# Row pairs 0, 2, 4, 5 and 6 of each down product as seven block products, one weight sum by an accumulating GpSimd transfer

## The chip, the cores and the metric

The kernel runs on one core of a Trainium2 chip. The metric is the device time of one execution in microseconds (us). TensorE (PE) multiplies, VectorE (DVE) and ScalarE (ACT) do elementwise work, GpSimd (POOL) does a little of that and issues transfers, SyncE (SP) only issues transfers. Each engine works through its own queue in order and waits there on semaphores.

## The reference

One decoder layer for 256 tokens of width 1024, in float32: a gated FFN at half weight, a mixer of two attentions, a second gated FFN at half weight, a final norm.

```
h = x + 0.5 * swiglu(rms_norm(x, n1), gate1, up1, down1)     # hidden width 2816
h = h + hybrid_mixer(rms_norm(h, n2), ...)                   # w_in 1024 x 5120, two attentions, w_out
h = h + 0.5 * swiglu(rms_norm(h, n3), gate2, up2, down2)
out = rms_norm(h, final_norm)

swiglu(x, g, u, d) = (silu(x @ g) * (x @ u)) @ d
```

The case is about `(...) @ d`, the down product of each FFN: 256 x 2816 times 2816 x 1024.

## The kernel before

**Weights as a stream.** All weights come as 376 tiles of 128 x 512 float32, in the order in which they are used, two tiles to a chunk of 512 KB. SyncE loads chunks into four buffers (`raw`); a chunk's buffer is loaded anew when its last reader is done (`load`, L170, called at the end of `split`).

**Three matmuls a product.** A float32 product is made of two reduced parts for each factor: `wh` is the weight rounded to fp32r (ScalarE, L213 or with a gain L217), `wl` the rest (VectorE, L214 or L218). A product of a 128-token block and a weight tile is three matmuls, high by high, high by low, low by high (`mm3`, L353, and its lines 355 to 357). There are ten buffers for the pairs `wh`, `wl`.

**Splitting ahead.** After each product (`unit`, L359) the kernel calls `weave.tick()`, which gives the other tasks a step, and `W.pump()`, which splits at most one more weight. In a down product an item may be split when it is at most eight ahead of the item that TensorE uses (`AHEAD_DOWN`, 9), and when one of the ten buffers is free.

**Tasks in ticks.** A tick is one product. The activations of the hidden layer are transposed by VectorE in 32 x 32 squares, and 16 small transfers (`exchange`, L506) move the squares into place; some ticks later they are split into `hth` and `htl` (`turn_hidden`, L551). Blocks of hidden columns go in pairs p; the transfers for p = 4 and 5 are issued by GpSimd, the others by SyncE. So while the down product begins, GpSimd still issues the exchanges of the last two.

**Seven products for eight.** The down product takes the 22 rows of weight tiles in row pairs g = 0 to 10. A row pair is four tiles, B11, B12, B21, B22, and with two token blocks of two column blocks of activations it is a 2 x 2 by 2 x 2 block product: eight block products, or seven in Winograd's form. Pairs 0, 2, 4, 6 of each FFN use seven (`SEVENS`, L31), the others eight. For a seven, VectorE makes four sums of activations (L563 to L566, small, once for each pair, split into `c_f`) and four sums of weights, T3 to T6 (`seventh`, L187, its instruction L195):

```
T3 = B12 - B11,  T4 = B22 - B12,  T5 = B22 - T3,  T6 = B21 - T5
```

The seven weight operands are then B11, B21, B22, T3, T4, T5, T6, each split as any other weight: seven items where a plain row pair has four (each of these used twice). Their products go to X, (0,0), (0,1), V, Z, Y, (1,0) (`seven`, L656). X, Y, Z, V are summed over all sevens and added to h by VectorE after the last of them (`post`, L675, D_POST = 3 ticks later: L679 to L696, with ScalarE's copy of X at L683); the rest goes to the ordinary sums in PSUM.

**The order.** TensorE and SyncE run in the order of the program throughout. From the start to the end of the first FFN's down products (up to its last rows), and from early in the second FFN on, all engines do (`ordered`). Elsewhere a planner orders VectorE, ScalarE and GpSimd by its own costs. The first FFN ends with 7 rows (`TAILS`, 1: 7) that are taken for one half of the columns and then for the other, so that the residual (L652), the transposes of h (L431, `uq`), their exchange on GpSimd and SyncE and the split into `uh`, `ul` can run ahead of the mixer's first projection (`in`). The second FFN has the plain pairs 7 and 8 and a tail of 4 rows behind its last seven.

Of the kernel before, what the change touches and what calls it, by code (L numbers as in the profile page):

```python
# [8 lines left out]
F32 = mybir.dt.float32  # L9
# [18 lines left out]
NEG = -1e30  # L28
CH = 2
N_TILES = 376  # L30
SEVENS = (0, 2, 4, 6), (0, 2, 4, 6)  # L31
W_IN = FB * KD + 2 * KF + 3 * len(SEVENS[0])
W_BR = W_IN + 10 * KD
W_OUT = W_BR + 16
# [29 lines left out]
D_STICK = (7, 6, 6, 6)  # L64
AHEAD = 7
AHEAD_DOWN = 9


INV_FREQ = [
# [30 lines left out]
class Weave:  # L100


    def __init__(self):
        self.now = 0
        self.tasks = []
# [54 lines left out]
class Weights:  # L160


    def __init__(self, nc, pool, early, sums, stream, gain, bufs, ahead):
        self.early, self.sums, self.items = early, sums, _items()
        self.nc, self.pool, self.stream, self.gain = nc, pool, stream, gain
        self.bufs, self.ahead = bufs, ahead
        self.loaded = self.ready = self.freed = self.at = 0
        self.raw, self.parts, self.behind = {}, {}, {}

    def load(self, n, tiles=0):  # L170

        n = min(n, N_TILES // CH)
        while self.loaded < n * CH + tiles:
            c, j = divmod(self.loaded, CH)
            if j == 0:
                nm = f"raw{c}"
                self.raw[c] = self.early(nm) if c < 12 else self.pool.tile([P, CH * 512], F32, name=nm, tag="raw", bufs=4)
            step = 1 if c < 3 else CH
            s = slice(j * 512, (j + step) * 512)
            for piece in HALVES if self.loaded == 0 else (s,):  # L180
                self.nc.sync.dma_start(self.raw[c][:, piece], self.stream[c, :, piece])
            self.loaded += step

    def tile(self, s):
        return self.raw[s // CH][:, s % CH * 512:s % CH * 512 + 512]

    def seventh(self, s, j):  # L187

        if j < 4:
            if j == 0:  # L190
                self.made = {}
            a, b, o = ((1, 0, 3), (3, 1, 4), (3, 3, 5), (2, 5, 6))[j]
            self.made[o] = self.sums(f"T{s}_{o}")
            b = self.made[b] if j > 1 else self.tile(s + b)
            self.nc.vector.tensor_sub(self.made[o], self.tile(s + a), b)  # L195
        raw = self.made[j] if j > 2 else self.tile(s + (0, 2, 3)[j])
        return raw, {1: s // CH, 3: s // CH + 1}.get(j)

    def split(self):
        i = self.ready  # L200
        s, j = self.items[i]
        used = s // CH if s % CH == CH - 1 else None
        if j is None:
            self.load(s // CH + 1)
            raw = self.tile(s)
        else:
            self.load(s // CH + (2 if j else 1))
            raw, used = self.seventh(s, j)
        hi = self.pool.tile([P, 512], F32R, name=f"wh{i}", tag="wh", bufs=self.bufs)
        lo = self.pool.tile([P, 512], F32R, name=f"wl{i}", tag="wl", bufs=self.bufs)  # L210
        g = self.gain(i)
        if g is None:
            self.nc.scalar.copy(hi, raw)  # L213
            self.nc.vector.tensor_sub(lo, raw, hi.bitcast(F32))  # L214
        else:
            for s in HALVES if i == 0 else (slice(0, 512),):
                self.nc.scalar.activation(hi[:, s], raw[:, s], AF.Copy, scale=g)  # L217
                self.nc.vector.scalar_tensor_tensor(lo[:, s], raw[:, s], g, hi[:, s].bitcast(F32),  # L218
                                                    op0=ALU.mult, op1=ALU.subtract)
        self.parts[i] = hi, lo  # L220
        self.ready += 1
        if i in self.behind:
            self.behind.pop(i)()
        if used is not None:
            del self.raw[used]
            self.load(used + 1 + 4)
# [19 lines left out]
def hybrid_layer_kernel(ctx, tc, x, xt, pos, g_final, bgate, wstream, out):  # L246
# [19 lines left out]
    def big(nm, dt=F32R):  # L266
        return work.tile([P, 1024], dt, name=nm, tag="big", bufs=24)
# [7 lines left out]
    def row512(nm):  # L275
        return work.tile([P, 512], F32, name=nm, tag="tok", bufs=4)


    h = [consts.tile([P, D], F32, name=f"h{t}") for t in range(2)]
    first = consts.tile([P, 3 * KD + T], F32, name="first")  # L280
# [11 lines left out]
                return gk[:, n * KD + k:n * KD + k + 1]  # L292
        return None

    W = Weights(nc, wpool, lambda nm: big(nm, F32), row512, wstream, gain, WB, AHEAD0)

    xin = [big(f"xin{j}", F32) for j in range(2)]

# [112 lines left out]
    class Normed:  # L411
        def __init__(self, t, nm):
            self.t, self.nm = t, nm
            self.parts = big(f"{nm}h{t}"), big(f"{nm}l{t}")
            self.r = consts.tile([P, 1], F32, name=f"r_{nm}{t}")
            self.there = set()
# [112 lines left out]
    def ffn(base, xn, nm, on_half, lag, last=False):  # L529
# [21 lines left out]
        def turn_hidden(p, n):  # L551
            moved = big(f"hm_{nm}{p}", F32)
            yield from exchange(moved, squares[p], n, [nc.gpsimd if p > 3 else nc.sync], D_MOVE)
            yield D_MOVED
            hts[p] = big(f"hth_{nm}{p}"), big(f"htl_{nm}{p}")
            split(plain(hts[p][0][:, 0:n * P]), plain(hts[p][1][:, 0:n * P]), slots(moved, n))
            for g in range(2 * p, 2 * p + 2):
                if g in sevens:
                    a11, a21, a12, a22 = (slots(moved, n)[:, g % 2 * 4 + s] for s in range(4))
                    yield D_SUMS  # L560
                    raw = wide(f"cs_{nm}{g}", 512)
                    s1, s3, s2, s4 = (plain(raw)[:, s] for s in range(4))
                    nc.vector.tensor_add(s1, a21, a22)  # L563
                    nc.vector.tensor_sub(s3, a11, a21)
                    nc.vector.tensor_sub(s2, s1, a11)
                    nc.vector.tensor_sub(s4, a12, s2)  # L566
                    yield D_SUMS
                    both = big(f"c_{nm}{g}")
                    split(both[:, 0:512], both[:, 512:1024], raw)
                    crossed[g] = [[both[:, q * 512 + m * P:q * 512 + (m + 1) * P] for q in range(2)] for m in range(4)]  # L570
# [104 lines left out]
        def post():  # L675

            def add(t, c, src):
                s = slice(c * 512, c * 512 + 512)
                nc.vector.scalar_tensor_tensor(h[t][:, s], src, 0.5, h[t][:, s], op0=ALU.mult, op1=ALU.add)  # L679

            xs, w, r, wv = (row512(f"{q}_{nm}") for q in ("xs", "xy", "xyz", "xyv"))
            add(0, 0, common["X"])
            nc.scalar.copy(xs, common["X"])  # L683
            yield 1
            nc.vector.tensor_add(w, common["Y"], xs)
            yield 1
            nc.vector.tensor_add(r, common["Z"], w)
            yield 1
            add(1, 0, r)
            yield 1  # L690
            nc.vector.tensor_add(wv, common["V"], w)
            yield 1
            add(0, 1, wv)
            yield 1
            rv = row512(f"xyzv_{nm}")
            nc.vector.tensor_add(rv, common["V"], r)  # L696
            yield 1
            add(1, 1, rv)
# [564 lines left out]
```

## Time and profile before

| | |
|---|---|
| median of 3 runs | 548.29 us (548.05 to 548.39) |
| profiled execution, its own time | 548.34 us |
| its span, first to last instruction | 546.6 us |
| granted TensorE clock | 0.996 |
| TensorE busy | 99% |
| VectorE busy | 83% |
| ScalarE busy | 65% |
| GpSimd busy | 21% |
| moved by DMA | 112.23 MB, mean 205 GB/s |

How to read the lines of the profile. A group's line gives source line, engine, operation, output <- inputs by the program's names, shapes, count, then busy us and mean ns of one, then the idle time of the engine ahead of these instructions and what ended it. A line of the timeline gives start and duration in us, then the engine, line, operation, names, shapes, count, and in brackets the idle time before it with what ended it. A line of transfers gives the names, the issuing queue, count, size of one and the median time from issue to landing. A line of waits gives the waiting instruction <- what ended the wait, the total in us, the number of waits and the longest. A line of a window gives its bounds, its length, the busy us of the engine with the number of instructions, the granted clock, the busy share of the DMA engines and their GB/s. Matmuls overlap in the pipeline, so their durations are longer than the distance between their starts.

### The profile page before, as it was taken

Reading aid. Unit: us, or ns where it says so; the run is one execution under the profiler, and the core shown is the slowest. Engines: PE = TensorE matmul, PEld = TensorE weight load, DVE = VectorE, ACT = ScalarE, POOL = GpSimd, SP = SyncE. Lnnn points to the kernel's source line nnn. Section 1 sums busy time; section 2 is a strip of 40 time slices with the busy share of each in tenths; the row PEclk is TensorE's granted clock in tenths of the full one; section 3 lists DMA queues with packets and bytes.
Section 4 is the critical chain, followed back from the end, with each engine's and each line's share of the span. In section 5 each row is a group of like instructions: output and inputs, shape, how many; then the busy total and the mean of one; then the engine's idle time right before and its main releaser. Section 6 shows DMA issues by size and latency. Waiting matters only on the chain.

```text
span 546.6 us, 8039 instructions
## 1 busy us (share of the span) xinstructions
PE 539.1 (99%) x2466; PEld 445.5 (82%) x2466; DVE 452.2 (83%) x803; ACT 357.0 (65%) x612; POOL 114.3 (21%) x225
## 2 busy tenths in 40 slices
PE   9999999999999999999999999999999999999995
PEld 6888888888888888888888888888888888888884
DVE  5797799889999776889888888877677878899985
ACT  6775666657754866677876775466666566667653
POOL 2410000036103846032022200383000000353000
PEclk9999999999999999999999999999999999999998
DMA  8957766685666766455555363687667766758532
GB/s 279 406 181 240 236 210 207 205 257 177 232 212 199 253 223 201 156 160 181 180 151 174 126 209 135 201 269 220 224 187 232 221 222 205 228 166 260 201 109 77
DMA packets 42619, 112.23 MB, mean 205 GB/s; under 512 B 8352, under 2 KB 16080, under 8 KB 42576
## 3 DMA queue, kind: packets, MB, share of 16 engines
q1 hardware_dynamic: 37824, 106.82, 58.9%
q0 software_dynamic: 4464, 4.55, 3.1%
q8 instruction: 19, 0.31, 0.2%
q10 hardware_dynamic: 288, 0.36, 0.2%
q14 instruction: 24, 0.20, 0.1%
HBM read 102.25 MB, written 1.05 MB: 189 GB/s over the span
## 4 chain that ended last, share of the span: by engine, by line
PE 99%; ACT 0%; DVE 0%; issue 0%; ACTq 0%
PE gu_f L357 13%; PE gu_f L356 13%; PE gu_f L355 13%; PE in L355 7%; PE in L357 7%; PE in L356 7%; PE dn_f L356 5%; PE dn_f L357 5%; PE dn_f L355 5%; PE wo L357 1%; PE wo L355 1%; PE wo L356 1%; PE gu_f L368 1%; PE gu_f L369 1%; PE gu_f L371 1%; PE y_b L962 1%
## 5 line engine op out<-in xcount | busy, mean ns | idle before, releaser
L218 DVE SCALAR_TENSOR_TENSOR wl<-raw,first,wh 128x512 fp32r<-128x512 f32 (+1 forms) x257 | 182.7, 746 | 34.9 <-ACT wh L217 34.2
L217 ACT ACTIVATE wh<-raw,first 128x512 fp32r<-128x512 f32 (+1 forms) x257 | 172.8, 716 | 47.0 <-PE gu_f L357 25.7
L213 ACT CAST wh<-raw 128x512 fp32r<-128x512 f32 x112 | 64.8, 619 | 22.6 <-DMA raw<-in_wstream 5.7
L214 DVE TENSOR_TENSOR wl<-raw,wh 128x512 fp32r<-128x512 f32 x112 | 73.9, 693 | 3.9 <-ACT wh L213 3.7
L511 POOL DMA_DIRECT2D hm_f<-hs_f x64 | 31.6, 501 | 203.9 <-ACT wh L217 186.7
L355 PE MATMUL gu_f<-wh,zh 128*128 128x512 f32 x176 | 68.5, 389 | 0.0
L356 PE MATMUL gu_f<-wl,zh 128*128 128x512 f32 x176 | 68.5, 389 | 0.0
L357 PE MATMUL gu_f<-wh,zl 128*128 128x512 f32 x176 | 68.5, 389 | 0.0
L355 PE MATMUL in<-wh,uh 128*128 128x512 f32 x160 | 63.5, 397 | 0.0
L357 PE MATMUL in<-wh,ul 128*128 128x512 f32 x160 | 62.5, 391 | 0.0
L356 PE MATMUL in<-wl,uh 128*128 128x512 f32 x160 | 62.4, 390 | 0.0
L355 PE MATMUL gu_f<-wh,xh 128*128 128x512 f32 x144 | 56.0, 389 | 0.0
L356 PE MATMUL gu_f<-wl,xh 128*128 128x512 f32 x144 | 56.0, 389 | 0.0
L357 PE MATMUL gu_f<-wh,xl 128*128 128x512 f32 x144 | 56.0, 389 | 0.0
L355 PE MATMUL dn_f<-wh,hth_f 128*128 128x512 f32 x124 | 48.3, 390 | 0.0
L357 PE MATMUL dn_f<-wh,htl_f 128*128 128x512 f32 x124 | 48.2, 389 | 0.0
L356 PE MATMUL dn_f<-wl,hth_f 128*128 128x512 f32 x124 | 48.2, 389 | 0.0
L355 PEld LDWEIGHTS gu_f<-wh,zh 128*128 128x128 f32 x176 | 33.0, 188 | 6.9
L356 PEld LDWEIGHTS gu_f<-wl,zh 128*128 128x128 f32 x176 | 33.0, 188 | 6.9
L357 PEld LDWEIGHTS gu_f<-wh,zl 128*128 128x128 f32 x176 | 33.0, 188 | 6.7
L357 PEld LDWEIGHTS in<-wh,ul 128*128 128x128 f32 x160 | 30.0, 188 | 6.5
L355 PEld LDWEIGHTS in<-wh,uh 128*128 128x128 f32 x160 | 30.1, 188 | 6.0
(320 smaller groups left out, 953.5 us busy)
## 6 DMA issues: line engine op xcount, KB each, us to landing
raw<-in_wstream SPq DMA_DIRECT2D x185, 512.0 KB, 4.2
hm_f<-hs_f SPq DMA_DIRECT2D x128, 32.0 KB, 3.9
raw<-in_wstream SPq DMA_DIRECT2D x5, 256.0 KB, 4.6
h<-in_x SPq DMA_DIRECT2D x2, 512.0 KB, 8.2
hm_f<-hs_f POOLq DMA_DIRECT2D x32, 32.0 KB, 3.6
bg<-in_bgate POOLq DMA_DIRECT2D x4, 256.0 KB, 4.8
xin<-in_xt SPq DMA_DIRECT2D x2, 256.0 KB, 6.7
hm_f<-hs_f POOLq DMA_DIRECT2D x32, 16.0 KB, 3.7
```

Of the source, the lines that this page charges most:

```text
L213: self.nc.scalar.copy(hi, raw)
L214: self.nc.vector.tensor_sub(lo, raw, hi.bitcast(F32))
L217: self.nc.scalar.activation(hi[:, s], raw[:, s], AF.Copy, scale=g)
L218: self.nc.vector.scalar_tensor_tensor(lo[:, s], raw[:, s], g, hi[:, s].bitcast(F32), op0=ALU.mult, op1=ALU.subtract)
L355: nc.tensor.matmul(o, ah, wh, start=first, stop=False)
L356: nc.tensor.matmul(o, ah, wl, start=False, stop=False)
L357: nc.tensor.matmul(o, al, wh, start=False, stop=last)
L368: nc.tensor.matmul(o, ah, wh, start=first, stop=False)
L369: nc.tensor.matmul(o, al, wh, start=False, stop=False)
L371: nc.tensor.matmul(o, ah, wl, start=False, stop=last)
L511: queues[m % len(queues)].dma_start(moved[j * w:j * w + w, i * n * w:(i + 1) * n * w], squares[i * w:i * w + w, j * n * w:(j + 1) * n * w])
L962: nc.tensor.matmul(o, v[j][p][:, pc], w[q], start=(i, j) == (0, 0), stop=i == 2, skip_group_check=True)
```

## The change

Pair 5 joins the sevens of each FFN. T3 is no longer made by VectorE but by two transfers that GpSimd issues: B11 from HBM into a buffer of its own, and then B12 from HBM with an addition onto it (`accum_op`). Since a transfer only adds, all signs are turned: T3 = B11 + B12, T4 = B22 + B12, T5 = B22 + T3, T6 = B21 + T5, with the activation sums and the final additions changed to match. The two transfers stand in GpSimd's queue where the 14th and the 9th item ahead of the pair's first is split (`AHEAD_LOAD`, `AHEAD_ADD`). The buffer is one of four that attention uses later (tag "r", `spare512`). The raw tiles themselves are still loaded as before, since B11 is an operand and B12 goes into T4.

```diff
-SEVENS = (0, 2, 4, 6), (0, 2, 4, 6)
+SEVENS = (0, 2, 4, 5, 6), (0, 2, 4, 5, 6)
+ADDED = 0,
+AHEAD_LOAD = 14
+AHEAD_ADD = 9
 class Weights:
+        self.made, self.ahead_of = {}, {}
+        for i, (s, j) in enumerate(self.items):
+            if j == 0:
+                for step, lead in enumerate((AHEAD_LOAD, AHEAD_ADD)):
+                    self.ahead_of.setdefault(i - lead, []).append((s, step))
...
+    def given(self, s, step):
+
+        for n in ADDED:
+            if step == 0:
+                self.made[s, 3 + n] = self.spare(f"T{s}_{3 + n}")
+                self.nc.gpsimd.dma_start(self.made[s, 3 + n], self.source(s + 3 * n))
+            else:
+                self.nc.gpsimd.dma_start(self.made[s, 3 + n], self.source(s + 1), accum_op=ALU.add)
+
     def seventh(self, s, j):
 
-        if j < 4:
-            if j == 0:
-                self.made = {}
-            a, b, o = ((1, 0, 3), (3, 1, 4), (3, 3, 5), (2, 5, 6))[j]
-            self.made[o] = self.sums(f"T{s}_{o}")
-            b = self.made[b] if j > 1 else self.tile(s + b)
-            self.nc.vector.tensor_sub(self.made[o], self.tile(s + a), b)
-        raw = self.made[j] if j > 2 else self.tile(s + (0, 2, 3)[j])
+        if 0 < j < 4 and not (j == 1 and 1 in ADDED):
+            a, b, o = ((3, 1, 4), (3, 3, 5), (2, 5, 6))[j - 1]
+            self.made[s, o] = self.sums(f"T{s}_{o}")
+            b = self.made[s, b] if j > 1 else self.tile(s + b)
+            self.nc.vector.tensor_add(self.made[s, o], self.tile(s + a), b)
+        raw = self.made.pop((s, j)) if j > 2 else self.tile(s + (0, 2, 3)[j])
         return raw, {1: s // CH, 3: s // CH + 1}.get(j)
 
     def split(self):
         i = self.ready
+        for args in self.ahead_of.pop(i, ()):
+            self.given(*args)
...
+    def spare512(nm):
+        return work.tile([P, 768], F32, name=nm, tag="r", bufs=4)[:, 0:512]
...
-                    nc.vector.tensor_add(s1, a21, a22)
+                    nc.vector.tensor_sub(s1, a22, a21)
                     nc.vector.tensor_sub(s3, a11, a21)
-                    nc.vector.tensor_sub(s2, s1, a11)
+                    nc.vector.tensor_add(s2, s1, a11)
                     nc.vector.tensor_sub(s4, a12, s2)
...
-                nc.vector.scalar_tensor_tensor(h[t][:, s], src, 0.5, h[t][:, s], op0=ALU.mult, op1=ALU.add)
+                nc.vector.scalar_tensor_tensor(h[t][:, s], src, -0.5 if c else 0.5, h[t][:, s], op0=ALU.mult, op1=ALU.add)
...
-            nc.vector.tensor_add(w, common["Y"], xs)
+            nc.vector.tensor_sub(w, xs, common["Y"])
```

More of the change, by code (lines that the diff above doesn't have):

```diff
@@ L160, with __init__ @@
 class Weights:
-    def __init__(self, nc, pool, early, sums, stream, gain, bufs, ahead):
-        self.early, self.sums, self.items = early, sums, _items()
+    def __init__(self, nc, pool, early, sums, spare, stream, gain, bufs, ahead):
+        self.early, self.sums, self.spare, self.items = early, sums, spare, _items()
         self.nc, self.pool, self.stream, self.gain = nc, pool, stream, gain
@@ L179, in load @@
             s = slice(j * 512, (j + step) * 512)
+            if {0, 1} <= set(ADDED) and (c * CH, 0) in self.items:
+                s = slice(0, 512)
             for piece in HALVES if self.loaded == 0 else (s,):
@@ L185, in tile, with source @@
         return self.raw[s // CH][:, s % CH * 512:s % CH * 512 + 512]
-    def seventh(self, s, j):
-        if j < 4:
-            if j == 0:
-                self.made = {}
-            a, b, o = ((1, 0, 3), (3, 1, 4), (3, 3, 5), (2, 5, 6))[j]
-            self.made[o] = self.sums(f"T{s}_{o}")
-            b = self.made[b] if j > 1 else self.tile(s + b)
-            self.nc.vector.tensor_sub(self.made[o], self.tile(s + a), b)
-        raw = self.made[j] if j > 2 else self.tile(s + (0, 2, 3)[j])
+    def source(self, s):
+        return self.stream[s // CH, :, s % CH * 512:s % CH * 512 + 512]
+    def given(self, s, step):
[5 more added lines that the diff above has]
+                self.nc.gpsimd.dma_start(self.made[s, 3 + n], self.source(s + 1), accum_op=ALU.add)
+    def seventh(self, s, j):
+        if 0 < j < 4 and not (j == 1 and 1 in ADDED):
[4 more added lines that the diff above has]
+        raw = self.made.pop((s, j)) if j > 2 else self.tile(s + (0, 2, 3)[j])
         return raw, {1: s // CH, 3: s // CH + 1}.get(j)
@@ L293, in gain @@
         return None
-    W = Weights(nc, wpool, lambda nm: big(nm, F32), row512, wstream, gain, WB, AHEAD0)
+    W = Weights(nc, wpool, lambda nm: big(nm, F32), row512, spare512, wstream, gain, WB, AHEAD0)
     xin = [big(f"xin{j}", F32) for j in range(2)]
```

## The prediction

> **What bounds the kernel now.** I read the page's engine table and its chain first, then the waits of TensorE.
>
> ```profile
> PE 539.1 (99%) x2466; PEld 445.5 (82%) x2466; DVE 452.2 (83%) x803; ACT 357.0 (65%) x612; POOL 114.3 (21%) x225
> PE 99%; ACT 0%; DVE 0%; issue 0%; ACTq 0%
> PE warm L346 <- DVE zeros L325: 1.1, 1, 1.1
> ```
>
> The chain is TensorE alone, and its only wait is at the start. Matmuls overlap, so the pace is not the 389 ns of one but the distance of starts. The view of the X and Y banks gives the first and last start of the X product, in pairs 0 and 6:
>
> ```profile
> L355 PE MATMUL dn_f1XY<-wh,hth_f x4: 389/389/389, 125.2 to 155.8; 128*128 128x512 f32 x4
> L355 PE MATMUL dn_f2XY<-wh,hth_f x4: 389/389/389, 482.7 to 513.3; 128*128 128x512 f32 x4
> ```
>
> Between them stand 45 products of three matmuls (pairs 7, 8, 7, 8, 7, 8): 30.6 us, so 0.68 us a product and 0.227 us a matmul, in both FFNs, without a gap. The profiled execution took 548.34 us for a span of 546.6 us; the median of the runs is 548.29, so the two agree to 0.05 us. I sum from 548.34.
>
> Who is next? The busy time of VectorE from the start of the down products to the first result taken from X, and the groups of the first stretch:
>
> ```profile
> 124.80:163.80 39.00, 38.93 (x67) 1.00 0.61 205
> 482.40:521.40 39.00, 38.93 (x66) 1.00 0.63 207
> L214 DVE TENSOR_TENSOR wl<-raw,wh 128x512 fp32r<-128x512 f32 x30 | 19.4, 689 | 0.0
> L214 DVE TENSOR_TENSOR wl<-T,wh 128x512 fp32r<-128x512 f32 x13 | 8.1, 685 | 0.0
> L195 DVE TENSOR_TENSOR T<-raw,T 128x512 f32<-128x512 f32 x6 | 4.1, 688 | 0.0
> L195 DVE TENSOR_TENSOR T<-raw 128x512 f32<-128x512 f32 x3 | 2.1, 687 | 0.0
> ```
>
> VectorE runs 39 us here without idling. It is a second bound that the whole-span 83% hides: whatever is added to it arrives later, and only the lead of the weights over TensorE pays for that.
>
> **What is removed.** One product of eight in pair 5 of each FFN, so 6 matmuls: 6 x 0.227 = 1.36 us, 0.68 in each FFN. If nothing waits: 548.34 - 1.36 = 546.98.
>
> **What VectorE gains and loses.** Operations of 128x512 follow each other faster than they last:
>
> ```profile
> 137.94 2.49 DVE L214 TENSOR_TENSOR wl<-raw,wh 128x512 fp32r<-128x512 f32 x4
> 140.34 0.69 DVE L195 TENSOR_TENSOR T<-raw 128x512 f32<-128x512 f32 x1
> 141.55 0.69 DVE L195 TENSOR_TENSOR T<-raw,raw 128x512 f32<-128x512 f32 x1
> ```
>
> Four starts in 2.40 us: 0.602 us each. Pair 5 splits seven operands instead of four tiles (+3 wl) and makes T4, T5, T6 (+3). T3 of pairs 2, 4 and 6 leaves the stretch (-3); T3 of pair 0 lay ahead of it, where VectorE idled anyway. Net +3 x 0.602 = +1.81 us on an engine with no idle time, while TensorE gets there 0.68 us sooner. The changed signs cost nothing, the counts being the same. The four column sums of pair 5 (0.93 us together) and their low half (0.60) come right behind pair 4's, near 106 us, and end in idle time, 0.98 and 1.14 us before the next two hidden blocks; TensorE takes nothing from them for 40 us:
>
> ```profile
> 105.68 0.29 DVE L563 TENSOR_TENSOR cs_f<-hm_f 128x128 f32<-128x128 f32 x1
> 106.61 1.41 DVE L218 SCALAR_TENSOR_TENSOR wl<-raw,first,wh 128x512 fp32r<-128x512 f32 x2
> 112.97 0.48 DVE L539 SCALAR_TENSOR_TENSOR sh_f<-gu_f,r_x,sh_f 128x256 f32<-128x256 f32 x1 [0.98 <-ACT sh_f L538]
> 115.07 0.48 DVE L539 SCALAR_TENSOR_TENSOR sh_f<-gu_f,r_x,sh_f 128x256 f32<-128x256 f32 x1 [1.14 <-ACT sh_f L538]
> ```
>
> ScalarE gains four casts for each FFN and has 35% idle: nothing.
>
> ```profile
> L213 ACT CAST wh<-T 128x512 fp32r<-128x512 f32 x32 | 19.7, 620 | 16.1 <-DVE T L195 11.8 <-PE gu_f L357 4.3
> ```
>
>
> **Where the lead is used up: pair 6.** The shortest lead late in the down products is that of T3 of pair 6.
>
> ```profile
> 154.72 2.50 DVE L214 TENSOR_TENSOR wl<-T,wh 128x512 fp32r<-128x512 f32 x4
> 158.04 0.39 PE L356 MATMUL dn_f1ZV<-wl,c_f 128*128 128x512 f32 x1
> ```
>
> Ready at 154.72 + 0.69 = 155.41, used at 158.04: 2.63 us. After the change 2.63 - 1.81 - 0.68 = 0.14 us. So the three pairs in a row just fit, if VectorE itself waits for nothing.
>
> **VectorE's own wait.** It could. T4 of pair 4 reads the second chunk of that pair, and the chunk's load starts when T6 of pair 2 is done:
>
> ```profile
> 135.68 0.33 SPq L181 DMA_DIRECT2D raw<-in_wstream  x1
> 141.43 1.14 ACT L213 CAST wh<-raw 128x512 fp32r<-128x512 f32 x2 [2.48 <-DMA raw<-in_wstream]
> raw<-in_wstream SPq DMA_DIRECT2D x185, 512.0 KB, 4.2
> ```
>
> ScalarE waited for it until 141.43, and T4 started at 141.55: no loss yet. After the change T4's turn comes at 141.55 - 1.20 = 140.35, and the load is issued at 135.68 - 0.60 = 135.08. With the median 4.2 us it lands at 139.3, and the wait w is nothing; if it lands again only at 141.4, T4 stays at 141.55, 1.2 us late. The added transfers can push it further: 512 KB, a load and an add, at the 205 GB/s for a share of 0.61 above (336 when the DMA is full) are 1.6 us, of which I put half ahead of this chunk. So w lies between 0 and 2.0; I take 0.6, the middle of the first two, since GpSimd, held by an add, issues fewer exchanges beside this load (below). In the second FFN the same T4 has its turn at 499.10 - 1.20 = 497.90 and its load is issued at 493.24 - 0.60: 5.3 us of room, between the 4.2 and the 5.7 us seen. Its w lies between 0 and 1.2 (0.4 late and half of the 1.6); I take 0.1.
>
> ```profile
> 499.10 0.69 DVE L195 TENSOR_TENSOR T<-raw,raw 128x512 f32<-128x512 f32 x1
> 493.24 0.33 SPq L181 DMA_DIRECT2D raw<-in_wstream  x1
> ```
>
> The row's rule is that a load beside others lands late (5.7 us, not 4.2). The Trainium skill says the same against this change: "DMA: Bandwidth & Descriptors", section "Issuing engines are not separate DMA queues", has all queues run on the same 16 DMA engines, so that moving a sum to GpSimd's queue does not move it off the loads' road. By that rule alone w would be nearer its upper end, and the sum about 1 us higher.
>
> **The seam behind the first FFN.** The delay of 1.81 + w does not end at pair 6. VectorE goes on without a pause that could be shortened: the result from X, one idle stretch that hangs on it (ScalarE's copy of X), the sums of the common products, the residual, the transposes of h for the next norm:
>
> ```profile
> 163.14 0.70 DVE L679 SCALAR_TENSOR_TENSOR h<-dn_f1XY,h 128x512 f32<-128x512 f32 x1
> 165.01 0.69 DVE L214 TENSOR_TENSOR wl<-raw,wh 128x512 fp32r<-128x512 f32 x1 [1.17 <-ACT wh L213]
> 169.22 0.68 DVE L652 SCALAR_TENSOR_TENSOR h<-dn_f,h 128x512 f32<-128x512 f32 x1
> 171.02 0.71 DVE L431 STREAM_TRANSPOSE uq<-h 128x512 f32<-128x512 f32 x1
> ```
>
> Behind them wait 16 exchange transfers on GpSimd's and SyncE's queues, then the split of u, then the first projection on TensorE:
>
> ```profile
> 181.75 0.69 DVE L387 TENSOR_TENSOR ul<-uq,uh 128x512 fp32r<-128x512 f32 x1 [0.51 <-DMA uq<-uq]
> 183.22 0.39 PE L357 MATMUL in<-wh,ul 128*128 128x512 f32 x1
> ```
>
> The low half is ready at 182.44 and used at 183.22: 0.78 us, 0.05 of which I leave for the signal, so 0.73. If the chain moves one for one, projection starts 1.81 + 0.6 - 0.73 = 1.68 us later than before, and the 0.68 saved ahead of it is lost within that. SP's loads between the exchanges wait for the same late splits, so they give nothing back.
>
> **The second FFN.** Pairs 7 and 8 follow as plain ones, and at the end VectorE idles 2.03 us for TensorE:
>
> ```profile
> 529.31 1.90 DVE L214 TENSOR_TENSOR wl<-raw,wh 128x512 fp32r<-128x512 f32 x3
> 534.61 0.69 DVE L652 SCALAR_TENSOR_TENSOR h<-dn_f,h 128x512 f32<-128x512 f32 x1 [2.03 <-PE dn_f L357]
> ```
>
> That idle time takes up 1.81 + 0.1, and pair 6 keeps 0.14 - 0.1. Here the 0.68 us is kept.
>
> **GpSimd's transfers.** The profile has no accumulating one. Nearest are a plain one of the same 256 KB from HBM on that queue, and one of twice the bytes, as an accumulation reads its destination too:
>
> ```profile
> bg<-in_bgate POOLq DMA_DIRECT2D x4, 256.0 KB, 4.8
> h<-in_x SPq DMA_DIRECT2D x2, 512.0 KB, 8.2
> 127.42 7.89 POOL L511 DMA_DIRECT2D hm_f<-hs_f  x16 [6.15 <-ACT wh L213]
> ```
>
> Between 4.8 and 8.2 us, then; I take 6. Each issue is 0.5 to 0.6 us of GpSimd. Ten pairs make 20 such transfers, 5 MB on 112. In its order the add for pair 4 stands five exchange issues behind 127.42, so about 130, landed by 136 to 138; T5 of pair 4, two operations behind T4, reads it at 141.55. The add for pair 5 waits for its load (issued about 132, landed 137); the exchanges behind it, up to ten, move from 138 to some 147, and their split comes at about 161. Pair 5's T3 lands by 144 to 146 and is read ten operations and a 1.14 us split behind pair 4's, at 148.7; pair 6's by about 150 to 153, read at 154.7. The price is nothing, with 2 us to spare even at 8.2. The four borrowed buffers serve attention 80 us later, and the tile for pair 5's column sums makes, by my count of the code, 24 of 24 in the second FFN: no wait.
>
> **The sum.** First FFN +1.68, second -0.68: +1.0 us, **549.3 us**, a slight loss of 0.18% that a measurement cannot tell from no change (0.2%, or 1.1 us, is about what it can).
>
> **Rivals.** *The full saving*: w is 0 and the seam does not move one for one, because the exchanges land sooner with fewer other transfers about or the order around them gives way: 546.98. For it: 10.7 of the 18.6 us from X to the split of u are transfers, whose times scatter. Against it: the 0.78 us. With w = 0 and the seam as counted, 548.34 + 1.08 - 0.68 = 548.7, no change either. *Slower*: w is 1.8 in the first FFN and 1.0 in the second, the added transfers falling among the chunks of pairs 4 to 6. First FFN 1.81 + 1.8 - 0.73 = +2.88; second -0.68 + (1.0 - 0.14) = +0.18: 551.4. It decides from w above 0.7. For it: the load that took 5.7 us. Against: the DMA engines' 61 to 63% share. *T3 late*: an accumulation of 14 us. The add for pair 5, issued about 138, lands at 152, and T5 waits 3.3 us in each FFN: 1.81 + 3.3 - 0.73 and -0.68 + 3.3 - 0.14, together +6.9, 555.2. Nothing in the profile speaks for such a length.
>
> **Chances.** As forecast, within 0.2% either way, 0.44. The full saving or most of it 0.16. Slower by more than 0.2%: 0.40, of which the late chunk 0.33, T3 or something else on GpSimd's queue 0.07. The range from 547.0 to 551.3 leaves out the late T3, the worst of the late chunks and the saving beyond the count. The forecast's own range is 548.3 to 550.2.
>
> **What would show it.** TensorE has 6 matmuls fewer, and VectorE makes 30 T where it made 32. VectorE's result from X must start near 165.0 + w, not 163.14; uq's first transposes near 172.8 + w; the first projection matmul near 184.4, not 182.76. T4 of pair 4 shows w. A chain that is TensorE alone, with the projection starting near 182.1, would make the seam wrong; a seam as counted and a pair 6 where TensorE waits more than 1 us would make w too small.

## The result, and the profile after

The changed kernel takes 555.34 us (median of 4 runs, 554.82 to 556.63), the kernel before 548.34 us on the same chip (548.05 to 548.39): a ratio of 1.0132, 95% interval 1.0114 to 1.0150. The forecast was 549.3 us and the range ended at 551.3. The change makes the kernel 7.0 us slower, and neither the forecast nor the range saw it. The profiled execution took 556.63 us for a span of 554.8 us; it is the slowest of the four, so the stages below add up to 8.2 us and not to 7.0.

The page of the changed kernel: the engines, the chain, the DMA queue of GpSimd, the transfers.

```profile
PE 542.5 (98%) x2460; PEld 442.9 (80%) x2460; DVE 457.4 (82%) x817; ACT 360.6 (65%) x620; POOL 127.7 (23%) x245
q0 software_dynamic: 6704, 9.79, 7.5%
PE 77%; DMA 9%; DVE 7%; issue 2%; POOL 2%; ACT 2%; SPq 0%; ACTq 0%; DVEq 0%; POOLq 0%
T<-in_wstream POOLq DMA_DIRECT2D x20, 256.0 KB, 6.4
hm_f<-hs_f POOLq DMA_DIRECT2D x32, 32.0 KB, 6.6
```

The six matmuls are gone (2460 for 2466). But the chain, TensorE to 99% before, now runs 9% through transfers and 7% through VectorE. A T transfer lands after 6.4 us, as forecast (6). The exchanges behind it on GpSimd's queue land after 6.6 us, where the page of before has 3.6.

Where TensorE is later than before, by the starts of its matmuls in the two traces:

| event | before | after | later by |
|---|---|---|---|
| X product of pair 0, first FFN | 125.18 | 125.51 | 0.33 |
| last down product of the first FFN | 182.54 | 185.60 | 3.06 |
| first matmul of the projection | 182.76 | 186.20 | 3.44 |
| its second token half | 188.67 | 194.16 | 5.49 |
| first X product, second FFN | 482.73 | 488.58 | 5.85 |
| last down product of the second FFN | 539.88 | 547.69 | 7.81 |
| end of the span | 546.63 | 554.78 | 8.15 |

So there are three places: the end of the first FFN, one jump of 2.05 us (5.49 - 3.44) inside the projection, and the second FFN. From the 49th matmul of the projection to the X product in the second FFN all kernels here take 288.5 to 288.7 us. The waits of TensorE from 120 to 210 us of the changed kernel:

```profile
PE in L380 <- ACT uh L411: 1.7, 2, 1.4
PE dn_f L381 <- DVE wl L236: 0.8, 3, 0.4
PE dn_f1ZV L381 <- DVE wl L236: 0.5, 2, 0.2
```

Before, this stretch had no wait. The waits are less than the loss: the matmul that waited 0.24 us at 158.88 starts 0.64 us behind the one ahead of it and the next one another 0.33 behind, where a matmul without a wait follows after 0.227. Counted by the starts in this way, pair 5 lost 1.2 us, pair 6 lost 1.2 and the last rows of the first FFN 0.8. And what these three wait for, in the timeline of the changed kernel (VectorE, ScalarE, GpSimd and TensorE, start and duration in us):

```profile
142.32 0.69 DVE L236 TENSOR_TENSOR wl<-raw,wh 128x512 fp32r<-128x512 f32 x1 [2.16 <-ACT wh L235]
...
167.77 0.68 DVE L704 SCALAR_TENSOR_TENSOR h<-dn_f1XY,h 128x512 f32<-128x512 f32 x1
...
192.65 0.21 POOL L908 TENSOR_SCALAR rq<-r_u 128x1 f32<-128x1 f32 x1
192.89 0.69 ACT L909 ACTIVATE qa<-in,rq 128x512 f32<-128x512 f32 x1 [2.03 <-POOL rq L908]
193.49 0.62 ACT L411 CAST uh<-uq 128x512 fp32r<-128x512 f32 x1
194.16 0.50 PE L380 MATMUL in<-wh,uh 128*128 128x512 f32 x1 [1.45 <-ACT uh L411]
...
504.57 0.69 DVE L236 TENSOR_TENSOR wl<-raw,wh 128x512 fp32r<-128x512 f32 x1 [1.35 <-ACT wh L235]
506.19 0.69 DVE L215 TENSOR_TENSOR T<-raw,raw 128x512 f32<-128x512 f32 x1 [0.92 <-DMA raw<-in_wstream]
```

VectorE, which had no idle time here before, waits 2.16 us in the first FFN and 1.35 + 0.92 = 2.27 us in the second, both times at pair 4, for its raw chunks (through ScalarE's rounding of the chunk, or by itself). This is the w of the prediction, and it is 2.16 and 2.27 where 0.6 and 0.1 were put in. At 192.89 ScalarE stands 2.03 us with qa, whose scale rq GpSimd makes at 192.65, and the rounding of u, for which TensorE waits, stands behind it. In the kernel before, this rounding came first:

```profile
187.07 0.62 ACT L386 CAST uh<-uq 128x512 fp32r<-128x512 f32 x1 [0.36 <-issue]
188.93 0.69 ACT L884 ACTIVATE qa<-in,rq 128x512 f32<-128x512 f32 x1 [1.24 <-PE in L357]
```

Why the raw chunk is late: busy time of each engine, then granted clock, share of the DMA engines and GB/s, from 136 to 142 us, and the raw loads of 130 to 146 us. Before:

```profile
136.00:139.00 3.00, 3.00 (x14) 2.46 (x14) 3.00 (x6) 2.94 (x6) 2.70 (x7) 1.00 0.70 241
139.00:142.00 3.00, 3.00 (x15) 2.49 (x14) 3.00 (x6) 0.57 (x2) 0.33 (x1) 1.00 0.64 210
raw<-in_wstream SPq DMA_DIRECT2D x7, 512.0 KB, 4.4
```

After:

```profile
136.00:139.00 3.00, 3.00 (x15) 2.49 (x14) 3.00 (x6) 1.90 (x5) 0.99 (x2) 1.00 1.06 377
139.00:142.00 3.00, 3.00 (x15) 2.49 (x14) 1.16 (x2) 0.69 (x2) 2.04 (x4) 1.00 0.98 315
raw<-in_wstream SPq DMA_DIRECT2D x7, 512.0 KB, 6.4
```

The DMA engines, at 0.64 to 0.70 before, are full. The seven raw loads take 6.4 us to landing at the median, where the same stretch of before has 4.4.

### The profile page after: what moved, and what is told of

It reads as the page before. It is cut to its first block, busy times and chain, and to the rows that moved or that the text cites. A ratio compares the mean times of both kernels' runs of the same rounds, so it can differ in the third digit from the quotient of the medians.

```text
span 554.8 us, 8092 instructions
## 1 busy us (share of the span) xinstructions
PE 542.5 (98%) x2460; PEld 442.9 (80%) x2460; DVE 457.4 (82%) x817; ACT 360.6 (65%) x620; POOL 127.7 (23%) x245
## 3 DMA queue, kind: packets, MB, share of 16 engines
q0 software_dynamic: 6704, 9.79, 7.5%
## 4 chain that ended last, share of the span: by engine, by line
PE 77%; DMA 9%; DVE 7%; issue 2%; POOL 2%; ACT 2%; SPq 0%; ACTq 0%; DVEq 0%; POOLq 0%
PE gu_f L381 12%; PE gu_f L382 12%; PE gu_f L380 12%; PE in L380 6%; PE in L382 6%; PE in L381 6%; DMA raw<-in_wstream 4%; DVE wl L236 3%; DMA hm_f<-hs_f 3%; DMA T<-in_wstream 2%; PE dn_f L381 1%; POOL hm_f L536 1%; PE wo L382 1%; PE wo L380 1%; PE wo L381 1%
## 5 line engine op out<-in xcount | busy, mean ns | idle before, releaser
L536 POOL DMA_DIRECT2D hm_f<-hs_f x64 | 35.3, 706 | 197.2 <-DMA hm_f<-hs_f 102.3
L235 ACT CAST wh<-raw 128x512 fp32r<-128x512 f32 x110 | 63.6, 618 | 24.7 <-DMA raw<-in_wstream 13.6
L236 DVE TENSOR_TENSOR wl<-raw,wh 128x512 fp32r<-128x512 f32 x110 | 72.1, 686 | 7.2 <-ACT wh L235 7.0
L381 PE MATMUL dn_f<-wl,hth_f 128*128 128x512 f32 x112 | 44.1, 393 | 0.2 <-DVE wl L236 0.2
L380 PE MATMUL dn_f<-wh,hth_f 128*128 128x512 f32 x112 | 43.7, 390 | 0.0
L382 PE MATMUL dn_f<-wh,htl_f 128*128 128x512 f32 x112 | 43.7, 390 | 0.0
```

Source lines behind the costliest of these rows:

```text
L380: nc.tensor.matmul(o, ah, wh, start=first, stop=False)
L381: nc.tensor.matmul(o, ah, wl, start=False, stop=False)
L382: nc.tensor.matmul(o, al, wh, start=False, stop=last)
L536: queues[m % len(queues)].dma_start(moved[j * w:j * w + w, i * n * w:(i + 1) * n * w], squares[i * w:i * w + w, j * n * w:(j + 1) * n * w])
```

## Experiments

In each result the number in brackets is the 95% interval of the ratio to the kernel before, whose median beside these runs was 548.28 to 548.43 us. "Run 5" is experiment 5; waits at pair 4 are VectorE's, summed over its raw chunks. A loss "by the starts" is counted as above. Of the four or more runs of a kernel one is profiled, so a difference between two profiled runs can differ from that of the medians.

**1. T3 back on VectorE, five sevens, no transfers.**

```diff
-ADDED = 0,
+ADDED = ()
-        if 0 < j < 4 ...:
-            a, b, o = ((3, 1, 4), (3, 3, 5), (2, 5, 6))[j - 1]
+        if j < 4:
+            a, b, o = ((1, 0, 3), (3, 1, 4), (3, 3, 5), (2, 5, 6))[j]
```

> The changed kernel with its five seven-product pairs, but T3 = B12 - B11 made by VectorE like the other three sums: no T transfers at all. VectorE then does +7 operations per FFN against the kernel before (4.21 us at 0.602) instead of +3 (1.81 us). Theory L (the loss of the changed kernel is: the raw chunk of pair 4 late by 2.5 us because the T transfers take the DMA engines; VectorE's added work passed on one for one; about 2.0 us at the projection's second token half, where ScalarE's copy of the rows waits in front of the rounding): pair 4 finds its raw chunk, w goes back to 0 to 0.6; pair 6 comes 4.21 - 0.68 - 2.63... that is, its lead of 2.63 less 4.21 less 0.68 leaves TensorE waiting about 2.3 us in each down stage; result from X in the first FFN near 165.0 + 2.4 = 167.4 (against 167.77 changed), first projection matmul at 182.76 + 4.21 - 0.73 = 186.2, the 2.0 at the second half stays, second FFN +1.6: 548.3 + 3.5 + 2.0 + 1.6 = about 555.4. Rival V (VectorE's work is cheap in itself and only the transfers hurt): w gone and no stall at pair 6, 548.3 - 1.36 + 2.0 = about 549.

Measured: 557.19 us, 1.0158 (1.0141 to 1.0175). VectorE's result from X in the timeline of this kernel:

```profile
167.86 0.68 DVE L704 SCALAR_TENSOR_TENSOR h<-dn_f1XY,h 128x512 f32<-128x512 f32 x1
```

and the waits of TensorE over the whole span:

```profile
PE dn_f L381 <- DVE wl L236: 1.7, 7, 0.3
PE in L380 <- ACT uh L411: 1.7, 1, 1.7
```

VectorE waits for nothing at pair 4, and yet takes the result from X at 167.86, where the changed kernel does at 167.77. Seven operations more (7 x 0.602 = 4.21 us) come to the same as three operations and a wait of 2.16 us (3.97): the four operations that the transfers took off VectorE in this stretch came back as a wait. Rival V, 549 us, falls. Theory L falls short by 1.8 us: the second FFN lost 2.9 us in the stage, not 1.6, as its tail stalls too. The stall at the projection is here without any transfer.

**2. The transfers with four sevens.**

```diff
-SEVENS = (0, 2, 4, 5, 6), (0, 2, 4, 5, 6)
+SEVENS = (0, 2, 4, 6), (0, 2, 4, 6)
```

> Four seven-product pairs as before (0, 2, 4, 6) in both FFNs, T3 of each by the plain and the accumulating GpSimd transfer: so VectorE has 4 operations fewer per FFN than before (-2.41 us), TensorE the same 2466 matmuls, and the DMA engines 16 transfers of 256 KB more. Theory L: at pair 4 VectorE is as early as in the changed kernel and the raw chunk as late, so w is about 2.5; with pair 6's saving behind it VectorE ends at -2.41 + 2.5 = +0.1 us; no matmul waits, the order on ScalarE at the projection is that of before: 548.0 to 548.7. Rival T (the transfers cost TensorE time in some other way, for example by the exchanges behind them on GpSimd's queue): at 550 or above.

Measured: 550.43 us (549.50 to 552.07), 1.0043 (1.0026 to 1.0060). The profiled run, at 549.5 the fastest of the five, shows VectorE's waits at pair 4 at 0.79 us in the first FFN (0.36 and 0.43) and 1.91 in the second, where theory L had 2.5; the result from X is at 162.78, 0.4 us early (theory L: 0.1 late). Behind the start TensorE waits 0.2 us in all. Both FFNs take as long as before, and 0.85 of the 1.2 us that this run is longer fall into the first 48 matmuls of the projection (see 11). The other runs are up to 2.6 us longer, and none of them has a profile. Theory L is 1.7 us too low at the median; what costs that stays open.

**3. The second transfer plain.** The kernel leaves out the subtraction in T3, which then holds B12 alone.

```diff
-                self.nc.gpsimd.dma_start(..., self.source(s + 1), accum_op=ALU.add)
+                self.nc.gpsimd.dma_start(..., self.source(s + 1))
```

> The changed kernel, its second T transfer a plain copy of B12 in place of the accumulating one (the subtraction of B11 in T3 is left out, so T3 holds B12 alone). Bytes from HBM, number of transfers, their queue, their waits and every engine's instructions are the same. In the changed trace a packet of the accumulating transfer has 2048 bytes and takes about 195 ns, one of the plain transfer 4096 bytes and about 170 ns. If it is the accumulation's packets that hold up the raw chunk of pair 4 (1.56 us of each DMA engine against 0.68): w falls from 2.5 to about 1.6 in both FFNs and the time to 555.3 - 2 x 0.9 = about 553.5. If it is the bytes or the second queue as such: w stays at 2.5, 555.0 to 555.6.

Measured: 555.14 us (553.94 to 555.89), 1.0121 (1.0104 to 1.0138), so by the time alone the second answer. The trace says otherwise: VectorE's waits at pair 4 are 1.09 and 0.41 us in place of 2.16 and 2.27, T lands after 5.2 us, not 6.4, and the result from X starts at 166.80, 1.0 earlier. What ate it is TensorE's clock behind the stall at the projection. Windows of this kernel:

```profile
194.00:196.00 2.00, 2.00 (x6) 1.42 (x6) 0.49 (x2) 0.72 (x1) 1.71 (x6) 0.60 0.02 6
196.00:198.00 2.00, 2.00 (x7) 1.59 (x6) 1.44 (x2) 1.25 (x2) 1.34 (x3) 0.55 0.00 0
```

The granted clock (third number from the end) is 0.60 and 0.55 over these 4 us (0.50 in each finer window from 194.4 to 197.8), with 13 matmuls where the changed kernel makes 18 at 1.00. That is 1.6 us: from the start of the second half to its 25th matmul it takes 7.43 us, 5.83 in the changed kernel. The two runs with a mean clock of 0.993 took 555.64 and 555.89 us, those with 0.996 and 0.997 took 553.94 and 554.65. So this run could not tell; run 9 asks again without the stall.

**4. The transfers early.** The first four pairs' T3 is fetched ahead of the down stage, while its four buffers are free.

```diff
...
+        firsts = [(i, s) for i, (s, j) in enumerate(self.items) if j == 0]
+        for f in range(2):
+            mine = [x for x in firsts if (x[0] > 200) == (f == 1)]
+            for n, (i, s) in enumerate(mine):
+                at = mine[0][0] - 44 + 8 * n if n < 4 else mine[n - 4][0] + 7
+                for step in range(2):
+                    self.ahead_of.setdefault(at + 4 * step, []).append((s, step))
```

> The changed kernel with the T transfers of the first four seven-product pairs moved ahead of the down stage: the load of pair 0 at 44 stationary items before the stage, the next three 8 items apart, each add 4 items behind its load; pair 6's, for which a buffer comes free only then, at 7 items behind pair 0's first. Same instructions on every engine, same bytes. Theory L: the raw chunk of pair 4 is not held up (w 0 to 0.6 in both FFNs); VectorE's +1.81 stays, pair 6 just fits (lead 0.14), result from X near 165.5 to 166; first projection matmul near 184.2; the 2.0 at the second token half stays, as that is an order on ScalarE: first FFN and seam +1.1 to 1.7 and 2.0, second FFN -0.7 to 0: 550.7 to 552. Rival S (the transfers delay as much wherever they stand, or VectorE alone makes the stall): 554.5 or above.

Measured: 554.03 us, 1.0111 (1.0089 to 1.0133): better than the changed kernel by 1.3 us at the medians (the two intervals overlap), but neither theory's number. The timeline of VectorE:

```profile
141.32 0.69 DVE L218 TENSOR_TENSOR T<-raw,raw 128x512 f32<-128x512 f32 x1 [0.65 <-DMA raw<-in_wstream]
...
166.03 0.69 DVE L239 TENSOR_TENSOR wl<-raw,wh 128x512 fp32r<-128x512 f32 x1 [0.48 <-ACT wh L238]
166.64 0.68 DVE L707 SCALAR_TENSOR_TENSOR h<-dn_f1XY,h 128x512 f32<-128x512 f32 x1
```

The wait at pair 4 falls from 2.16 to 0.65 us, about the 0.6 that was allowed for (1.04 in the second FFN, more than that), but a new one of 0.48 stands at the end, and the result from X is 3.50 us later than before, not the 2.4 to 2.9 that were counted. By the starts, TensorE then loses not only 0.9 us at pair 6 but also 1.4 us in the tail (175 to 179 us), where the four splits that stand behind the X results on VectorE had a lead of 1.8 to 2.3 us before. That tail was in no step of mine.

**5. The order on ScalarE put back.**

```diff
+            done = split(...)
+            if self.nm == "u":
+                marks["uh"] = done.ins
...
+                    with tc.issue_after(marks["uh"]):
+                        nc.scalar.activation(dst, ps, AF.Copy, scale=rq[t])
```

> The changed kernel with one order put back as it was in the kernel before: on ScalarE the copy of the first projection's rows (qa from in, scaled by rq, which waits until GpSimd has made rq at 192.65) stands behind the rounding of the second token half (uh from uq) and no longer ahead of it. Nothing else. In the changed trace uh starts at 193.49 behind qa at 192.89, its last transfer was issued at 187.9 and such a transfer lands 3.5 later at the median, so uh could start near 191.4, TensorE's second half near 192.3 and not at 194.16. Theory O (this order costs its share of the loss): 555.3 less 1.6 to 2.05 = 553.3 to 553.7. Rival U (the rounding's input is as late as the copy): 555 or above.

Measured: 554.18 us, 1.0104 (1.0090 to 1.0117), 1.2 us less than the changed kernel by the medians, 2.2 between the profiled runs (554.42 and 556.63). ScalarE in this kernel:

```profile
191.30 0.62 ACT L411 CAST uh<-uq 128x512 fp32r<-128x512 f32 x1 [0.56 <-DMA uq<-uq]
193.10 0.69 ACT L913 ACTIVATE qa<-in,rq 128x512 f32<-128x512 f32 x1 [1.19 <-POOL rq L911]
```

The rounding starts at 191.30 (191.4 expected), the second half 6.30 us behind the first, 7.96 in the changed kernel: 1.66 us. In this stage that is theory O, at the low end of its 1.6 to 2.05; the whole is 0.5 us above its 553.7. U falls.

**6. Early and in order.** Edits 4 and 5 together.

> The transfers early (554.0) and the order on ScalarE put back, both. Theory O: the two add: 554.0 less 1.6 to 2.05 = 552.0 to 552.4. What is left over the kernel before is then VectorE's work in the down stages. Rival U: 553.5 or above.

Measured: 551.95 us, 1.0069 (1.0056 to 1.0083). The two add: 2.1 us below run 4, 2.2 below run 5.

**7. And without pair 5's sums.** The kernel leaves out T4, T5 and T6 of pair 5 in both FFNs; the products that need them read T3.

```diff
...
+        light = s in self.light
-        if 0 < j < 4 and not (j == 1 and 1 in ADDED):
+        if 0 < j < 4 and not light and not (j == 1 and 1 in ADDED):
-        raw = self.made.pop((s, j)) if j > 2 else ...
+        raw = self.made[s, 3] if light and j > 2 else self.made.pop((s, j)) if j > 2 else ...
```

> The kernel with early transfers and the order put back, and of pair 5 in both FFNs the three sums T4, T5, T6 on VectorE left out (its products 3 to 6 read T3 in their place, so these four products have other data and the same shapes): VectorE has the operations of the kernel before in number, TensorE the 2460 matmuls, the transfers stay. Theory S (with the transfers and the order out of the way, VectorE's 3 added operations of 0.602 us per FFN are what is left; in the first FFN each goes through to the seam, and adjacent pairs 5 and 6 leave no plain pair in which VectorE could get ahead): the stall at pair 6 (0.9) and in the tail (1.4) go, the result from X is 1.8 earlier than with the sums, so the first projection starts 0.2 to 1.0 late and the second FFN keeps 0.4 to 0.7 of its saving: 548.0 to 549.2. Rival N (the number of VectorE's operations is not it, but the order of its work or late raw chunks): above 550.5.

Measured: 548.53 us (10 runs), 0.9999 (0.9990 to 1.0008): theory S, in the middle of its range. Six operations of 0.602 us, 3.6 us of VectorE, moved the end by 3.42 us at the medians and by 2.79 between the profiled runs (551.63 and 548.84): 1.85 in the first FFN, where three of them are 1.81, and 0.96 in the second. The result from X, in the kernel of run 6:

```profile
166.04 0.68 DVE L710 SCALAR_TENSOR_TENSOR h<-dn_f1XY,h 128x512 f32<-128x512 f32 x1
```

in this one:

```profile
164.03 0.68 DVE L712 SCALAR_TENSOR_TENSOR h<-dn_f1XY,h 128x512 f32<-128x512 f32 x1
```

and all that is left of TensorE's waits behind the start:

```profile
PE dn_f2ZV L386 <- DVE wl L241: 0.2, 1, 0.2
PE in L385 <- ACT uh L416: 0.2, 1, 0.2
```

So 2.0 us for three operations (1.81) and a wait that went with them (0.16).

**8. One seven more, in the second FFN alone, on VectorE alone.** From the kernel before:

```diff
-SEVENS = (0, 2, 4, 6), (0, 2, 4, 6)
+SEVENS = (0, 2, 4, 6), (0, 2, 4, 6, 8)
```

> The kernel before with one more pair of seven products in the second FFN alone, pair 8, which has a plain pair on either side of it; T3 by VectorE, no T transfers; nothing else changed. TensorE does 3 matmuls less (0.68 us), VectorE 4 + 3 operations more (4.2 us, of which 7 x 0.602 with T3) in a stage whose result from X stands later and has no projection behind it. Theory D (it is the neighbourhood of pairs 5 and 6, and the seam behind the first FFN, that turn VectorE's work into time): the saving shows, 548.3 - 0.68 = 547.6, down to 547.3 and up to 548.3. Rival A (VectorE's added work goes through one for one in the second FFN too): 548.3 - 0.68 + 2 to 4.2 less a lead near 2 = 549.6 to 551.8.

Measured: 551.54 us, 1.0057 (1.0044 to 1.0070): rival A. TensorE waits nowhere in the down products and ends them at 539.09, 0.8 us earlier than before. The end of the span is 3.0 us later all the same. VectorE's additions to h, before:

```profile
531.12 1.47 DVE L652 SCALAR_TENSOR_TENSOR h<-dn_f,h 128x512 f32<-128x512 f32 x2
534.61 0.69 DVE L652 SCALAR_TENSOR_TENSOR h<-dn_f,h 128x512 f32<-128x512 f32 x1 [2.03 <-PE dn_f L357]
```

and in this kernel, with the chain on its page:

```profile
536.71 1.89 DVE L652 SCALAR_TENSOR_TENSOR h<-dn_f,h 128x512 f32<-128x512 f32 x3
PE 92%; DVE 3%; DMA 2%; ACT 1%; issue 1%; SPq 0%; DVEq 0%; ACTq 0%
```

The pair costs VectorE more than the seven operations that were expected: the page has 815 operations for 803, as pair 8's four column sums and their split (1.53 us) come at 508 to 511 us, where VectorE has no idle time either. 4.21 + 1.53 = 5.74 us, and the first of the three additions is 5.59 us later (536.71 for 531.12). The third waited 2.03 us for TensorE before; here it waits for nothing, stands behind VectorE's own work at about 537.9, 3.3 us later, and the end is 3.0 later. So the added work is passed on almost one for one until it meets idle time, which takes up 2.03 us of it.

**9. Order put back, and the second transfer plain.** Edits 5 and 3.

> The order on ScalarE put back (554.2), and the second T transfer plain, not accumulating (the subtraction of B11 in T3 left out; instructions, bytes from HBM and queue the same). With the order of the changed kernel the same edit took VectorE's waits in the first FFN from 2.16 to 1.10 us and in the second from 2.26 to 0.41, but the whole by 0.2 us only, because TensorE ran at a granted clock of 0.55 to 0.60 for 4 us behind the longer stall at the seam; that stall is gone here. Theory A (the accumulating packets, 2048 bytes in about 195 ns, hold up the raw chunks): first FFN 0.6 to 1.0 less, second 1.4 to 1.9 less: 551.3 to 552.2. Rival B (bytes and queue, not the accumulation): 553.8 to 554.5.

Measured: 552.52 us, 1.0072 (1.0057 to 1.0087), 1.7 us below run 5. Nearer to theory A, 0.3 above its end. VectorE's waits at pair 4 go from 1.68 to 1.44 us in the first FFN and from 1.96 to 0.88 in the second. In the first FFN the result from X starts at 167.54 in both kernels; the second FFN is 1.44 us shorter. So the addition in the transfer is a good part of the cost in the second FFN; in the first it shows in run 3 (X 1.0 us earlier than in the changed kernel) and not here.

**10. Pair 1 in place of pair 5.** From run 5's kernel:

```diff
-SEVENS = (0, 2, 4, 5, 6), (0, 2, 4, 5, 6)
+SEVENS = (0, 1, 2, 4, 6), (0, 1, 2, 4, 6)
```

> The changed kernel with the order on ScalarE put back (554.2) and pair 1 as seven products in place of pair 5, in both FFNs; transfers at the changed kernel's distances, counts of all instructions the same. The six operations of the added pair then stand ahead of VectorE's wait for the raw chunks of pair 4 and not behind it, so that the wait (1.7 us in the first FFN, 2.0 in the second) runs while VectorE still has work; pair 6 has plain pairs in front of it. Theory W (wait and work do not add when the work comes first): result from X near 163.14 + 1.81 + 0.6 = 165.6 in place of 167.5, no stall at pair 6; first FFN 1.5 to 2 less, second 1.3 to 1.9 less: 550.3 to 551.4. Rival P (the place of the pair is indifferent; the raw chunks come as much later): 553.5 to 554.5.

Measured: 552.76 us, 1.0080 (1.0065 to 1.0095), between the two. VectorE:

```profile
145.24 0.69 DVE L215 TENSOR_TENSOR T<-raw,raw 128x512 f32<-128x512 f32 x1 [1.36 <-DMA raw<-in_wstream]
...
166.38 0.68 DVE L707 SCALAR_TENSOR_TENSOR h<-dn_f1XY,h 128x512 f32<-128x512 f32 x1
```

The work ahead of pair 4 makes VectorE arrive later there, but the chunk lands later too (its buffer is given back by the same VectorE), so that of 1.68 us of wait 1.36 are left; in the second FFN 0.45 of 1.96. The stall is not gone but moved: TensorE now waits 1.1 us at pairs 1 and 2 of the first FFN and as much in the second. By the traces the first FFN is 1.3 us shorter than in run 5 and the second 0.15. Half of theory W by the time.

**11. The same T transfers in the kernel before, read by nothing; and four sevens with early transfers.**

```diff
+                self.nc.gpsimd.dma_start(self.dead[s], self.source(s))
+                self.nc.gpsimd.dma_start(self.dead[s], self.source(s + 1), accum_op=ALU.add)
```

> The kernel before, with the same 20 T transfers (load and accumulating add, at the same distances, pairs 0, 2, 4, 5, 6) into spare buffers that nothing reads; T3 stays with VectorE, four sevens, no other edit. Theory C: the raw chunks of pair 4 come as late as in the changed kernel, but VectorE gets there 1.8 us later, as it made T3 of pairs 0, 2 and 4 itself, so its wait is 0.3 to 0.8 in each FFN, which the lead of 0.73 at the seam and of 2.63 at pair 6 take up: 548.3 to 549.2. Rival Q: 550 or above.

Measured: 549.02 us (10 runs), 1.0011 (1.0001 to 1.0020): theory C. VectorE's wait from 136 to 172 us:

```profile
DVE T L216 <- DMA raw<-in_wstream: 1.4, 1, 1.4
```

and the result from X in the timeline:

```profile
164.66 0.68 DVE L705 SCALAR_TENSOR_TENSOR h<-dn_f1XY,h 128x512 f32<-128x512 f32 x1
```

With no other edit than transfers that nothing uses, VectorE waits 1.4 us at pair 4 (0.8 was the most I expected) and X is 1.5 us later. The lead at the seam takes up half of it.

> The four pairs of before with T3 by transfers (which took 550.4, VectorE having 4 operations less per FFN), now with the transfers ahead of the down stage, the last pair's at 7 items behind the first's. Theory C (what the transfers cost there, they cost by standing among the raw chunks of the down stage): 548.2 to 548.9. Rival Q (they cost wherever they stand, as GpSimd's queue or HBM is busy with them): 550 or above.

Measured: 549.87 us (10 runs), 1.0022 (1.0013 to 1.0032). Between the two; the early place is worth 0.6 us by the medians of this and run 2, whose intervals overlap. VectorE has no wait left in the first FFN and X is at 161.75, 1.4 us early, yet the 49th matmul of the projection starts 1.3 us later than before (0.25 us of it at the start of the down products). TensorE's waits there are 0.3 us on h and 0.2 on ul. By the starts these two waits are the whole of it: the matmuls start 0.67 and 0.61 us behind the ones ahead of them, and with the slower next ones that is 1.0 us. In run 2 the same two places cost 0.8. h and ul both come from VectorE, in the stretch that the planner orders; what made them late is not settled. An engine that is early did not make the seam early.

## Why the prediction was wrong

**What bounds the kernel: right, and it should have decided.** "VectorE runs 39 us here without idling" is what runs 1, 7 and 8 measure. In run 7, six operations are 3.42 us at the medians and 2.79 in the traces; in run 8, 5.74 us of work come through but for the idle time of 2.03 that they meet.

**The removed products: right in number.** TensorE has 6 matmuls fewer. But 0.68 us less of TensorE is worth something only where VectorE isn't late, and that was nowhere in the changed kernel.

**VectorE's net +3 operations: right.** From the hidden block at 124 us to the result from X there are 67 operations before and 70 after. The result's 163.14 becomes 167.77: 0.33 for a later start, 1.81, 2.16 of wait, and 0.33 in slower starts behind that wait and in rounding. The forecast was 165.0 + w.

**The term w failed, and it is the step that put the forecast outside its range.** It was bounded by 2.0 and 1.2 us and taken at 0.6 and 0.1; it measured 2.16 and 2.27. Three things in that step were wrong. I priced load and add by their bytes at the rate of the other loads, 1.6 us of all DMA engines. Of the queue's packet time (7.5% of 16 engines for 554.8 us, 5.7% of 553.9 with the add made plain, 3.1% of 546.6 without transfers) an estimate gives (505 - 271) / 20 = 11.7 us of engine time for a plain transfer and (666 - 271 - 117) / 10 = 27.8 us for an accumulating one, together 2.5 us of all 16 engines a pair. I looked at the second chunk of pair 4, and in the first FFN the first one was late. And I took the low part of the bounds, since GpSimd would issue fewer exchanges beside the load, and held the 61 to 63% share of the DMA engines against a late chunk. GpSimd did issue fewer (13 from 130 to 146 us, 18 before), but four T transfers came with them; and a mean share says little of a stretch in which transfers come in a heap, as the full windows show. The rule of the Trainium skill cited there ("DMA: Bandwidth & Descriptors", section "Issuing engines are not separate DMA queues") had the side that the trace now agrees with: w at its upper end, though not the size, since the upper end was too low. With the measured w the prediction's own sum is 548.34 + (1.81 + 2.16 - 0.73) + (-0.68 + 2.27 - 0.14) = 553.0, out of the range by this term alone; with the 2.05 us inside the projection, which the sum put at nothing, it is 555.1.

**The lead of pair 6: right as worked out, gone by w.** 0.14 us of lead against 2.16 of wait; the X product of pair 0 to the end of pair 6's takes 36.53 us, 34.68 before, in spite of a product less. By the starts TensorE loses 1.2 us at pair 6, and already 1.2 at pair 5: the sign that the prediction named ("a pair 6 where TensorE waits more than 1 us would make w too small").

**The seam: one for one, as forecast, and a second loss that was not.** The split of u is 4.43 us later (186.18 for 181.75) and the matmul that needs it 3.71 later (186.93 for 183.22), a lead of 0.72 for my 0.73. But the order behind it was taken as given. Wherever the first FFN has five sevens and nothing else orders it (the changed kernel, runs 1, 3 and 4), qa stands ahead of the rounding of the second half; with four sevens (runs 2, 8 and 11) it stands behind. The order costs 1.2 us (run 5) to 2.1 (run 6 against run 4). That the planner's own due times moved it there is an inference; what it costs is shown.

**The second FFN: wrong.** "Here the 0.68 us is kept" needed w near 0.1. With 2.27 us, pair 6 stalls, and 1.96 us were lost in the stage and 0.34 behind it. Run 7 against run 6 shows that VectorE's operations cost here too, about 1.0 us of the 2.8 in the traces.

**T3's transfers: right in themselves.** They land after 6.4 us for 6, and no split of a T3 waits for one. They cost through what else waits for the DMA engines. So the rival *T3 late* did not happen, and that its 555.2 lies next to the measured time is chance.

The runs add up, each step on top of the one before it, by the medians: order 1.16 us (run 5), early transfers 2.23 (run 6 against run 5), VectorE's six operations 3.42 (run 7), together 6.81 of the 7.0 us lost. The profiled runs give other sizes, and the places (first FFN: from the X product of pair 0 to the first matmul of the projection; second: from its first X product to its last down product; the rest of a row lies ahead of and behind these):

| step, us | first FFN | first 48 matmuls of the projection | second FFN | whole execution |
|---|---|---|---|---|
| order put back | +0.22 | -1.85 | -0.02 | -2.21 |
| transfers early | -1.76 | -0.15 | -1.07 | -2.79 |
| pair 5's sums left out | -1.85 | -0.04 | -0.96 | -2.79 |

What is left in run 7, 1.5 us above the full saving of 546.98, has VectorE's waits of 0.56 and 2.01 us at pair 4 beside it; that they cause it is not shown. The rival called *Slower* had the mechanism and less than half of the size. No kernel here beats the one before.

## What to carry to other kernels

When the stage has a second engine without idle time, count a removed product as nothing until that engine's own change is paid for: here six of its operations, 3.6 us, were worth 2.8 to 3.4 us at the end, and added work was absorbed only where the engine had idle time of its own (2.03 us in run 8). Work that is moved from such an engine to a transfer comes back as a wait when the same engine also waits for loads; price it in time of all DMA engines in that stretch, not at the mean share, and look at the order that a planner makes anew behind the edit.

## What the hardware showed that was not expected

An accumulating transfer of 256 KB took about 2.4 times the DMA engine time of a plain one (27.8 for 11.7 us, the estimate above; 6704 packets of that queue against 6064 with the add made plain, 64 more for each add). The packet times that the expectation of run 3 gives, 128 of 195 ns and 64 of 170, come to 25 and 11 us.

TensorE's granted clock was 0.50 from 194.4 to 197.8 us, behind a wait of 1.68 us (run 3), and stayed at 1.00 at the same place in the changed kernel behind a wait of 1.45 and in run 1 behind one of 1.66. The Trainium skill ("TensorE: Matmul & The Clock Gate", section "What's actually happening") has the array go to half rate after an idle window of about 3.4 us. This trace agrees in the half rate; the wait behind which it came was shorter, so here the length of one wait does not tell whether the clock falls.
